# Strassen-like projection groups: the second sum of weight quarters made by an adding DMA onto the first quarter's tile, with three of the sums of h negated

## The chip, the cores and the metric

The kernel runs on one core of one Trainium2 chip. The metric is the device time of one execution in microseconds (us); the figures are the median of three runs and, for everything read from the trace, one profiled execution. The engines are PE (matrix products), DVE (vector), ACT (scalar), POOL (general purpose, here used mostly to issue adding DMAs) and SP (issues the plain loads). TensorE's granted clock is given as a share of its full level of 2.4 GHz.

## The reference

The input x has 512 rows of 1024 channels. One layer: an RMS norm, one large projection with w_in (1024 to 12 x 1024 columns), three parallel branches, a gated merge, an output projection and a last norm.

```python
h = rmsnorm(x, norm_g[l])
proj = jnp.einsum('bsd,dn->bsn', h, w_in[l])
a_u, a_v, a_z, b_p, b_z, c_h, c_b, c_c, c_z, gate_logits = jnp.split(proj, SPLIT_OFFSETS, axis=-1)
ya = spatial_gating(gelu(a_u), gelu(a_v), ...) * silu(a_z)
yb = multiscale_pool(b_p, ...) * silu(b_z)
yc = c_b * causal_depthwise_conv(c_c * c_h, conv_w[l], conv_b[l]) * silu(c_z)
merged = sum over the branches of sigmoid(gate) * einsum(y, w_branch)
x = x + einsum(merged, w_out[l]);  return rmsnorm(x, final_g)
```

## The kernel before

**Products.** fp32 values are split into a high part (`whi`, `b11h`, made by a cast on ACT, line 59) and a rest (`wlo`, `b11l`, made by a subtraction on DVE, line 60); a product is three PE passes, high x high, high x rest, rest x high.

**Groups.** Eleven of the twelve blocks of 1024 columns of w_in (all but a_v) are computed in two groups each, 22 in all, by the generator `group`. A group has 2 x 256 output columns (halves `nh`) and the whole contraction of 1024 (halves `kh`), for 512 tokens (halves T1, T2). It takes seven products of quarter size instead of eight (a scheme of Strassen's kind). The fixed operands are quarters of h and their sums, made once by `sum_form`: b11, b21, b22, t1, t2, t3, t4. The weights are quarters `a11`, `a12`, `a21`, `a22` of 512 KB and sums of them. One product (`product`, line 444) is 24 matmuls of 256 columns on a weight tile of 128 x 1024.

**Order within a group.** `run` interleaves the groups: the first product of the next group (b11) stands ahead of the last two of this one (b22, t4). In the order of the code: b11 | b21, t2, t1, t3 | (b11 of the next group) b22, t4. The PSUM bank px takes b11, t2, t3 and t4 in turn; after each of the first three it is copied out by ACT (`copied`, line 450) before the next product is added to it. The order of each engine's instructions is fixed when the kernel is built, by a scheduler that keeps to the dependences and the buffers.

**Weights.** SP loads a11, a12, a21, a22 into tiles of the pool `wraw` (7 buffers, line 64) and the quarter (0,1) once more into `s1` (pool `wsum`, 2 buffers, line 468); POOL issues a DMA that adds the quarter (1,1) onto s1 in flight (line 469). DVE makes the other sums in place (line 457): a21 = a11 - a21, a11 = s1 - a11, a12 = a12 - a11. Every weight tile is then split by ACT and DVE into `whi` and `wlo`, which have 4 buffers each, so that the split of a product can begin when the product four places ahead of it has been read by PE.

**The rest.** Groups are mixed with other products (`proj`, matmuls of 512 columns, lines 105 to 107), with pooling windows (lines 677 to 684) and the convolution (lines 763 to 766) on DVE and ACT. The output projection at the end (lines 800 to 899) already makes its weight sums with adding DMAs (line 813).

Of the kernel before, what the change touches and what calls it, by code (L numbers as in the profile page):

```python
# [16 lines left out]
S = 512  # L17
# [13 lines left out]
def mixers_kernel(ctx, tc, x, norm_g, w_in, sgu_ln_g, sgu_ln_b, sgu_w, sgu_b, pool_w, pool_b, pool_scale,  # L31
# [22 lines left out]
    def bank():  # L54
        return psum.tile([P, 512], F32, tag="ps", name="ps")
# [284 lines left out]

    def sum_form(name, tag, out, in0, in1):
        nc.vector.tensor_tensor(out=out, in0=in0, in1=in1, op=ALU.subtract)
        moving[name] = form_tile(name, tag)
        split(*moving[name], out)


    sum_form("t1", "f3", b11, b12, b11)
    sum_form("t3", "f4", b12, b22, b12)
    sum_form("t2", "f5", b22, b22, b11)


# [48 lines left out]

    sum_form("t4", "f6", b21, b21, b22)

# [20 lines left out]
    def pair_of(ap):  # L423
        return ap.rearrange("p (j t) -> p j t", j=2)

    def group(c0, g, ct, use=None):
# [4 lines left out]
        def quarter(kh, nh):  # L431
            return load_raw(source(kh, nh), [4, GC])
# [19 lines left out]

        def plus(half, ts, s, ps):
            nc.vector.tensor_tensor(out=ct[:, half, :, ts], in0=pair_of(ps), in1=s, op=ALU.add)  # L454

        def sub(out, in0, in1, op=ALU.subtract):
            nc.vector.tensor_tensor(out=out, in0=in0, in1=in1, op=op)  # L457

        a11 = quarter(0, 0)
        f = halved(a11)  # L460
        px, py, pz = bank(), None, None
        product(f, "b11", px, True)
        yield
        c1 = copied(px)
        a12 = quarter(1, 0)
        f = halved(a12)
        s1 = wsum.tile([P, 4, GC], F32, tag="wsum", name="s1")
        nc.sync.dma_start(out=s1, in_=source(0, 1))
        nc.gpsimd.dma_start(out=s1, in_=source(1, 1), accum_op=ALU.add)  # L469
        a21, a22 = quarter(0, 1), quarter(1, 1)  # L470
        py = bank()
        product(f, "b21", py, True)
        plus(0, T1, c1, py)
        sub(a21, a11, a21)
        sub(a11, s1, a11)
        product(halved(a11), "t2", px, False)
        c2 = copied(px)
        pz = bank()
        product(halved(s1), "t1", pz, True)
        product(halved(a21), "t3", px, False)  # L480
        c3 = copied(px)
        sub(a12, a12, a11)
        plus(1, T2, c3, pz)
        yield
        product(halved(a12), "b22", pz, False)
        plus(0, T2, c2, pz)
        if use:
            use(ct[:, 0], 0, slice(0, S))
            use(ct[:, 1, :, T2], 1, T2)
        product(halved(a22), "t4", px, False)  # L490
        if use:
            use(pair_of(px), 1, T1)
        else:
            nc.scalar.copy(out=ct[:, 1, :, T1], in_=pair_of(px))
        yield

    def run(items):
# [22 lines left out]
        finish()  # L520

    def act_into(ct, func):
        def use(src, half, ts):
            nc.scalar.activation(out=ct[:, half, :, ts], in_=src, func=func)
        return use
# [216 lines left out]
    def branch_c(g):  # L742
# [6 lines left out]
        def conv_in():  # L749
            c["cc"] = out_tile("cc")  # L750

            def use(src, half, ts):
                nc.vector.tensor_mul(out=pads[half][:, :, PAD + ts.start : PAD + ts.stop], in0=src,
                                     in1=c["ch"][:, half, :, ts])

            yield from group(OFF["cc"], g, c["cc"], use)
# [12 lines left out]
        def gate_in():  # L769
            c["cb"] = out_tile("cb")  # L770

            def use(src, half, ts):
                y1 = c["cc"][:, half, :, ts]
                nc.vector.tensor_mul(out=y1, in0=src, in1=y1)

            yield from group(OFF["cb"], g, c["cb"], use)
# [27 lines left out]
    def source(n, k, u):  # L804
        r = k * HALF + u * 2 * P
        return w_out[r : r + 2 * P, n * HALF : (n + 1) * HALF].rearrange("(k p) c -> p k c", p=P)
# [118 lines left out]
```

## Time and profile before

| | |
|---|---|
| median of 3 runs | 702.57 us (701.31 to 703.35) |
| the profiled execution | 701.71 us |
| its span in the trace | 699.9 us |
| PE busy | 684.6 us (98%), weight loads 637.2 us (91%) |
| DVE, ACT, POOL busy | 530.6 us (76%), 343.3 us (49%), 53.4 us (8%) |
| mean granted clock of TensorE | 0.996 |

The span runs from the first to the last instruction of the trace; about 2 us of the execution lie around it. Busy time of an engine is the time in which it has an instruction under way; for PE, whose matmuls overlap, it says only that there was always one in flight.

### The profile page before, as it was taken

Reading aid. Unit: us, or ns where it says so; the run is one execution under the profiler, and the core shown is the slowest. Engines: PE = TensorE matmul, PEld = TensorE weight load, DVE = VectorE, ACT = ScalarE, POOL = GpSimd, SP = SyncE. Lnnn points to the kernel's source line nnn. Section 1 sums busy time; section 2 is a strip of 40 time slices with the busy share of each in tenths; the row PEclk is TensorE's granted clock in tenths of the full one; section 3 lists DMA queues with packets and bytes.
Section 4 is the critical chain, followed back from the end, with each engine's and each line's share of the span. In section 5 each row is a group of like instructions: output and inputs, shape, how many; then the busy total and the mean of one; then the engine's idle time right before and its main releaser. Section 6 shows DMA issues by size and latency. Waiting matters only on the chain.

```text
span 699.9 us, 11608 instructions
## 1 busy us (share of the span) xinstructions
PE 684.6 (98%) x4814; PEld 637.2 (91%) x4814; DVE 530.6 (76%) x615; ACT 343.3 (49%) x417; POOL 53.4 (8%) x68
## 2 busy tenths in 40 slices
PE   8999999999999999989999999999999999999994
PEld 6779999999899899989989899999999999898883
DVE  6997679695669667995855666798869975646995
ACT  7543546664244344655614334555645465244553
POOL 3112000000000000000000000000000000002112
PEclk9999999999999999999999999999999999999998
DMA  7974344746265434627617235556665543278733
GB/s 275 309 169 120 121 122 102 213 109 181 79 163 152 149 87 132 175 90 195 197 32 209 91 104 167 149 144 167 176 168 163 163 140 124 81 270 189 149 60 121
DMA packets 94457, 105.12 MB, mean 150 GB/s; under 512 B 3324, under 2 KB 85316, under 8 KB 94404
## 3 DMA queue, kind: packets, MB, share of 16 engines
q1 hardware_dynamic: 80020, 87.60, 38.9%
q0 software_dynamic: 13792, 15.73, 14.4%
q10 hardware_dynamic: 592, 1.05, 0.4%
q8 instruction: 37, 0.61, 0.4%
q14 instruction: 16, 0.13, 0.1%
HBM read 102.27 MB, written 2.10 MB: 149 GB/s over the span
## 4 chain that ended last, share of the span: by engine, by line
PE 89%; DVE 5%; DMA 2%; ACT 1%; issue 1%; POOL 0%; SPq 0%; POOLq 0%; ACTq 0%; DVEq 0%
PE ps L444 58%; PE ps L106 8%; PE ps L107 8%; PE ps L105 8%; PE ps L833 5%; PE ps L265 2%; DVE wlo L60 1%; DMA x_in<-in_x 1%; DVE win L677 1%; DMA wraw<-in_w_in 1%; DVE wraw L457 1%; PE ps L563 1%; PE ps L215 0%; DVE sz L454 0%; DVE ylo L709 0%
## 5 line engine op out<-in xcount | busy, mean ns | idle before, releaser
L59 ACT CAST whi<-wraw 128x1024 fp32r<-128x1024 f32 (+1 forms) x174 | 180.6, 1040 | 262.0 <-PE ps L444 160.2
L60 DVE TENSOR_TENSOR wlo<-wraw,whi 128x1024 fp32r<-128x1024 f32 (+1 forms) x174 | 209.6, 1210 | 95.6 <-ACT whi L59 95.3
L105 PE MATMUL ps<-yhi,whi 128*128 128x512 f32 x208 | 81.0, 389 | 0.0
L107 PE MATMUL ps<-yhi,wlo 128*128 128x512 f32 x208 | 80.9, 389 | 0.0
L106 PE MATMUL ps<-ylo,whi 128*128 128x512 f32 x208 | 80.9, 389 | 0.0
L457 DVE TENSOR_TENSOR wraw<-wraw 128x1024 f32<-128x1024 f32 x44 | 53.4, 1220 | 16.3 <-DMA wraw<-in_w_in 16.3
L469 POOL DMA_DIRECT2D s<-in_w_in x22 | 28.8, 1308 | 482.1 <-DMA s<-in_w_in 81.9
L444 PE MATMUL ps<-b22h,whi 128*128 128x256 f32 x176 | 50.6, 288 | 0.5 <-DVE sz L454 0.5
L444 PE MATMUL ps<-b21h,wlo 128*128 128x256 f32 x176 | 49.4, 280 | 1.2 <-DVE wlo L60 1.2
L444 PE MATMUL ps<-t2h,wlo 128*128 128x256 f32 x176 | 49.4, 281 | 0.5 <-DVE wlo L60 0.5
L444 PE MATMUL ps<-t1h,whi 128*128 128x256 f32 x176 | 49.4, 281 | 0.4 <-ACT whi L59 0.4
L444 PE MATMUL ps<-t2h,whi 128*128 128x256 f32 x176 | 49.5, 281 | 0.1
L444 PE MATMUL ps<-t2l,whi 128*128 128x256 f32 x176 | 49.6, 282 | 0.0
L444 PE MATMUL ps<-b11l,whi 128*128 128x256 f32 x176 | 49.6, 282 | 0.0
L444 PE MATMUL ps<-t3l,whi 128*128 128x256 f32 x176 | 49.6, 282 | 0.0
L444 PE MATMUL ps<-t1l,whi 128*128 128x256 f32 x176 | 49.6, 282 | 0.0
L444 PE MATMUL ps<-b22l,whi 128*128 128x256 f32 x176 | 49.6, 282 | 0.0
L444 PE MATMUL ps<-t4l,whi 128*128 128x256 f32 x176 | 49.6, 282 | 0.0
L444 PE MATMUL ps<-b21l,whi 128*128 128x256 f32 x176 | 49.6, 282 | 0.0
L444 PE MATMUL ps<-t3h,whi 128*128 128x256 f32 x176 | 49.3, 280 | 0.0
L444 PE MATMUL ps<-b22h,wlo 128*128 128x256 f32 x176 | 49.3, 280 | 0.0
L444 PE MATMUL ps<-b21h,whi 128*128 128x256 f32 x176 | 49.3, 280 | 0.0
(224 smaller groups left out, 1849.6 us busy)
## 6 DMA issues: line engine op xcount, KB each, us to landing
wraw<-in_w_in SPq DMA_DIRECT2D x96, 512.0 KB, 4.0
s<-in_w_in SPq DMA_DIRECT2D x22, 512.0 KB, 3.6
s<-in_w_in POOLq DMA_DIRECT2D x22, 512.0 KB, 6.3
wraw<-in_w_out SPq DMA_DIRECT2D x10, 512.0 KB, 3.8
wraw<-in_w_branch_a SPq DMA_DIRECT2D x8, 512.0 KB, 3.7
wraw<-in_w_branch_b SPq DMA_DIRECT2D x8, 512.0 KB
wraw<-in_w_branch_c SPq DMA_DIRECT2D x8, 512.0 KB
wraw<-in_w_out POOLq DMA_DIRECT2D x8, 512.0 KB, 6.0
```

Of the source, the lines that this page charges most:

```text
L59: keep(nc.scalar.copy(out=hi, in_=src))
L60: keep(nc.vector.tensor_tensor(out=lo, in0=src, in1=hi.bitcast(F32), op=ALU.subtract))
L105: nc.tensor.matmul(ps, lhsT=a[0], rhs=b[0], start=first, stop=False)
L106: nc.tensor.matmul(ps, lhsT=a[0], rhs=b[1], start=False, stop=False)
L107: nc.tensor.matmul(ps, lhsT=a[1], rhs=b[0], start=False, stop=last)
L265: pin(nc.tensor.matmul(vps[b], lhsT=a, rhs=r, start=done[b] == 1, stop=done[b] == 3 * KT))
L444: nc.tensor.matmul(ps[:, j * GC : (j + 1) * GC], lhsT=a[x][:, k, j * P : (j + 1) * P], rhs=moving[b][y][:, k, :], start=first and j == 0 a ...
L457: nc.vector.tensor_tensor(out=out, in0=in0, in1=in1, op=op)
L469: nc.gpsimd.dma_start(out=s1, in_=source(1, 1), accum_op=ALU.add)
L563: nc.tensor.matmul(mx[:, n * P : (n + 1) * P], lhsT=v_t[:, n, t * P : (t + 1) * P], rhs=wsT[:, t, :], start=True, stop=True)
L677: nc.vector.tensor_add(out=nxt[:, lo:], in0=cur[:, lo:], in1=cur[:, lo - step : PAD + S - step])
L833: nc.tensor.matmul(pss[b], lhsT=m_form[name][x_][:, k, b * P : (b + 1) * P], rhs=(hi, lo)[y_][:, k % 2, :], start=first and k == 0 and n == 0,
```

## The change

The group makes its second sum by a DMA too. s1 = (0,1) + (1,1) is used first, with -t1. DVE then adds a11 to s1 in place (line 481), which gives the operand for -t2, and adds that to a12 (line 486). When DVE has read a11, POOL issues a DMA that adds the quarter (0,1) from memory onto a11's tile (line 482); the tile then holds the operand for t3. The quarter a21 is no longer loaded into a tile of its own. Signs: the weight sums are now sums instead of differences, so t1, t2 and t4 are made with the opposite sign, and the uses of one output quarter get a sign (`plus`, `times`, `act_into`, a `scalar.mul` in place of a copy). The order of the products in the code is b21, -t1, -t2, t3 instead of b21, t2, t1, t3. Per group there are two DVE operations on weights instead of three, four loads by SP instead of five, and two adding DMAs instead of one.

```diff
@@ -338,15 +338,19 @@
     b11, b12, b22, b21 = (hsum[:, i] for i in range(4))
     moving = {"b11": hq[0, 0], "b21": hq[1, 0], "b22": hq[1, 1]}
 
-    def sum_form(name, tag, out, in0, in1):
-        nc.vector.tensor_tensor(out=out, in0=in0, in1=in1, op=ALU.subtract)
+    def sum_form(name, tag, out, in0, in1, sign=1.0):
+
+        if sign == 1.0:
+            nc.vector.tensor_tensor(out=out, in0=in0, in1=in1, op=ALU.subtract)
+        else:
+            nc.vector.scalar_tensor_tensor(out=out, in0=in0, scalar=sign, in1=in1, op0=ALU.mult, op1=ALU.subtract)
         moving[name] = form_tile(name, tag)
         split(*moving[name], out)
 
 
-    sum_form("t1", "f3", b11, b12, b11)
+    sum_form("-t1", "f3", b11, b11, b12)
     sum_form("t3", "f4", b12, b22, b12)
-    sum_form("t2", "f5", b22, b22, b11)
+    sum_form("-t2", "f5", b22, b22, b11, -1.0)
 
 
     ws_bs = outs.tile([P, 2, KT, P], F32, tag="outs", name="ws_bs")
@@ -398,7 +402,7 @@
         nc.vector.tensor_scalar(out=v_t[:, b, :], in0=v_t[:, b, :], scalar1=mv[:, 0:1], scalar2=rv,
                                 op0=ALU.subtract, op1=ALU.mult)
 
-    sum_form("t4", "f6", b21, b21, b22)
+    sum_form("-t4", "f6", b21, b22, b21, -1.0)
 
     def proj(w, j, rhs_hi, rhs_lo, nk=KT):
         ps = bank()
@@ -450,48 +454,50 @@
             nc.scalar.copy(out=s, in_=ps)
             return pair_of(s)
 
-        def plus(half, ts, s, ps):
-            nc.vector.tensor_tensor(out=ct[:, half, :, ts], in0=pair_of(ps), in1=s, op=ALU.add)
-
-        def sub(out, in0, in1, op=ALU.subtract):
-            nc.vector.tensor_tensor(out=out, in0=in0, in1=in1, op=op)
+        def plus(half, ts, s, ps, sign=1.0):
+            o = ct[:, half, :, ts]
+            if sign == 1.0:
+                nc.vector.tensor_tensor(out=o, in0=pair_of(ps), in1=s, op=ALU.add)
+            else:
+                nc.vector.scalar_tensor_tensor(out=o, in0=pair_of(ps), scalar=sign, in1=s, op0=ALU.mult,
+                                               op1=ALU.subtract)
 
         a11 = quarter(0, 0)
         f = halved(a11)
-        px, py, pz = bank(), None, None
+        px = bank()
         product(f, "b11", px, True)
         yield
         c1 = copied(px)
-        a12 = quarter(1, 0)
-        f = halved(a12)
         s1 = wsum.tile([P, 4, GC], F32, tag="wsum", name="s1")
         nc.sync.dma_start(out=s1, in_=source(0, 1))
         nc.gpsimd.dma_start(out=s1, in_=source(1, 1), accum_op=ALU.add)
-        a21, a22 = quarter(0, 1), quarter(1, 1)
+        a12 = quarter(1, 0)
+        f = halved(a12)
         py = bank()
         product(f, "b21", py, True)
         plus(0, T1, c1, py)
-        sub(a21, a11, a21)
-        sub(a11, s1, a11)
-        product(halved(a11), "t2", px, False)
+        pz = bank()
+        product(halved(s1), "-t1", pz, True)
+        nc.vector.tensor_tensor(out=s1, in0=s1, in1=a11, op=ALU.add)
+        nc.gpsimd.dma_start(out=a11, in_=source(0, 1), accum_op=ALU.add)
+        product(halved(s1), "-t2", px, False)
         c2 = copied(px)
-        pz = bank()
-        product(halved(s1), "t1", pz, True)
-        product(halved(a21), "t3", px, False)
+        a22 = quarter(1, 1)
+        nc.vector.tensor_tensor(out=a12, in0=a12, in1=s1, op=ALU.add)
+        product(halved(a11), "t3", px, False)
         c3 = copied(px)
-        sub(a12, a12, a11)
-        plus(1, T2, c3, pz)
+        plus(1, T2, c3, pz, 1.0 if use else -1.0)
         yield
         product(halved(a12), "b22", pz, False)
         plus(0, T2, c2, pz)
         if use:
-            use(ct[:, 0], 0, slice(0, S))
-            use(ct[:, 1, :, T2], 1, T2)
-        product(halved(a22), "t4", px, False)
+            use(ct[:, 0], 0, slice(0, S), 1.0)
+            use(ct[:, 1, :, T2], 1, T2, -1.0)
+        product(halved(a22), "-t4", px, False)
         if use:
-            use(pair_of(px), 1, T1)
+            use(pair_of(px), 1, T1, -1.0)
         else:
-            nc.scalar.copy(out=ct[:, 1, :, T1], in_=pair_of(px))
+            nc.scalar.mul(out=ct[:, 1, :, T1], in_=pair_of(px), mul=-1.0)
         yield
 
     def run(items):
@@ -519,9 +525,15 @@
                     after()
         finish()
 
+    def times(out, in0, in1, sign):
+        if sign == 1.0:
+            nc.vector.tensor_mul(out=out, in0=in0, in1=in1)
+        else:
+            nc.vector.scalar_tensor_tensor(out=out, in0=in0, scalar=sign, in1=in1, op0=ALU.mult, op1=ALU.mult)
+
     def act_into(ct, func):
-        def use(src, half, ts):
-            nc.scalar.activation(out=ct[:, half, :, ts], in_=src, func=func)
+        def use(src, half, ts, sign):
+            nc.scalar.activation(out=ct[:, half, :, ts], in_=src, func=func, scale=sign)
         return use
 
     def y_tiles():
@@ -749,9 +761,8 @@
         def conv_in():
             c["cc"] = out_tile("cc")
 
-            def use(src, half, ts):
-                nc.vector.tensor_mul(out=pads[half][:, :, PAD + ts.start : PAD + ts.stop], in0=src,
-                                     in1=c["ch"][:, half, :, ts])
+            def use(src, half, ts, sign):
+                times(pads[half][:, :, PAD + ts.start : PAD + ts.stop], src, c["ch"][:, half, :, ts], sign)
 
             yield from group(OFF["cc"], g, c["cc"], use)
 
@@ -769,9 +780,9 @@
         def gate_in():
             c["cb"] = out_tile("cb")
 
-            def use(src, half, ts):
+            def use(src, half, ts, sign):
                 y1 = c["cc"][:, half, :, ts]
-                nc.vector.tensor_mul(out=y1, in0=src, in1=y1)
+                times(y1, src, y1, sign)
 
             yield from group(OFF["cb"], g, c["cb"], use)
 
```

How it stands in the engines' order. All three places are in branch c, between the groups of block cc and block cb. ACT: s1_4386 is the weight sum of cc's group, wraw_4295 its a11, wraw_4389 its a12, wraw_4482 its a22; wraw_4517 is a11 of cb's group, and `part` tiles are copies of px. First the change:

```order
L59 CAST whi_4422<-s1_4386 128x1024
L454 COPY part_4384<-ps_4301 128x512
L59 CAST whi_4452<-s1_4386 128x1024
L500 ACTIVATE ch_4130<-ps_4137 128x2x256
L59 CAST whi_4485<-wraw_4295 128x1024
L59 CAST whi_4519<-wraw_4517 128x1024
L59 CAST whi_4548<-wraw_4389 128x1024
L59 CAST whi_4579<-wraw_4482 128x1024
L454 COPY part_4480<-ps_4301 128x512
```

and before (s1_4418, wraw_4321, wraw_4421 and wraw_4412 are the sum, a11, a21 and a12 of cc's group; wraw_4545 is a11 of cb's):

```order
L59 CAST whi_4453<-wraw_4321 128x1024
L450 COPY part_4410<-ps_4327 128x512
L59 CAST whi_4484<-s1_4418 128x1024
L59 CAST whi_4512<-wraw_4421 128x1024
L494 COPY ch_4154<-ps_4161 128x2x256
L59 CAST whi_4547<-wraw_4545 128x1024
L59 CAST whi_4576<-wraw_4412 128x1024
L450 COPY part_4481<-ps_4327 128x512
```

In the change the cast of the tile that the new DMA writes (whi_4485) stands ahead of the cast for the next group's first product (whi_4519) and of two more, and the copy of px after -t2 (part_4480) stands behind all of them; before, the tile wraw_4421 in that place was a DVE result.

PE at the same place. ps_4301 is px of cc's group, ps_4523 that of cb's; before they are ps_4327 and ps_4551, and ps_4483 is pz. The change, at the end of -t2:

```order
L448 MATMUL ps_4301<--t2h_433,whi_4452 128x256
L448 MATMUL ps_4301<--t2l_434,whi_4452 128x256
L448 MATMUL ps_4301<--t2h_433,wlo_4453 128x256
L448 MATMUL ps_4523<-b11h_163,whi_4519 128x256
L448 MATMUL ps_4523<-b11l_164,whi_4519 128x256
L448 MATMUL ps_4523<-b11h_163,wlo_4520 128x256
L448 MATMUL ps_4523<-b11h_163,whi_4519 128x256
```

and before, at the end of t1:

```order
L444 MATMUL ps_4483<-t1h_423,whi_4484 128x256
L444 MATMUL ps_4483<-t1l_424,whi_4484 128x256
L444 MATMUL ps_4483<-t1h_423,wlo_4485 128x256
L444 MATMUL ps_4327<-t3h_428,whi_4512 128x256
L444 MATMUL ps_4327<-t3l_429,whi_4512 128x256
L444 MATMUL ps_4327<-t3h_428,wlo_4513 128x256
```

Before, t1 with its 24 rows lies between t2 and t3, which share a bank, and the next group's b11 comes after t3. In the change b11 comes right behind -t2, and after 13 rows of it the 24 rows of t3 follow, then the other 11 of b11. From the first row of one b11 to that of the next there are 168 rows; the last row of b11 is the 48th, and -t1 begins with the 121st, -t2 with the 145th.

DVE one group later: cb's weight sum s1_4622, and the convolution (L775, L777; before L764, L766) of the block cc. The change:

```order
L532 SCALAR_TENSOR_TENSOR ppad1_1961<-cc_4294,ch_4130 128x2x256
L481 TENSOR_TENSOR s1_4622<-s1_4622,wraw_4517 128x1024
L486 TENSOR_TENSOR wraw_4625<-wraw_4625,s1_4622 128x1024
L460 TENSOR_TENSOR cc_4294<-ps_4421,part_4480 128x2x256
L532 SCALAR_TENSOR_TENSOR ppad1_1961<-ps_4301,ch_4130 128x2x256
L530 TENSOR_TENSOR ppad0_1959<-cc_4294,ch_4130 128x2x512
L775 SCALAR_TENSOR_TENSOR cc_4294<-ppad1_1961,pvec_442,cc_4294 128x512 x2
L775 SCALAR_TENSOR_TENSOR cc_4294<-ppad0_1959,pvec_442,cc_4294 128x512 x2
L777 SCALAR_TENSOR_TENSOR cc_4294<-ppad0_1959,pvec_442,cc_4294 128x512 x2
L777 SCALAR_TENSOR_TENSOR cc_4294<-ppad1_1961,pvec_442,cc_4294 128x512 x2
L460 TENSOR_TENSOR cb_4516<-ps_4631,part_4620 128x2x256
L60 TENSOR_TENSOR wlo_4689<-s1_4622,whi_4688 128x1024
```

and before (s1_4656 and wraw_4659 are the sum and a21 of cb's group, wraw_4783 is a11 of cz's):

```order
L454 TENSOR_TENSOR cc_4320<-ps_4483,part_4481 128x2x256
L60 TENSOR_TENSOR wlo_4723<-s1_4656,whi_4722 128x1024
L753 TENSOR_TENSOR ppad0_1969<-cc_4320,ch_4154 128x2x512
L753 TENSOR_TENSOR ppad1_1971<-ps_4327,ch_4154 128x2x256
L60 TENSOR_TENSOR wlo_4751<-wraw_4659,whi_4750 128x1024
L764 SCALAR_TENSOR_TENSOR cc_4320<-ppad0_1969,pvec_442,cc_4320 128x512 x2
L766 SCALAR_TENSOR_TENSOR cc_4320<-ppad0_1969,pvec_442,cc_4320 128x512 x2
L764 SCALAR_TENSOR_TENSOR cc_4320<-ppad1_1971,pvec_442,cc_4320 128x512 x2
L766 SCALAR_TENSOR_TENSOR cc_4320<-ppad1_1971,pvec_442,cc_4320 128x512 x2
L454 TENSOR_TENSOR cb_4544<-ps_4663,part_4648 128x2x256
L60 TENSOR_TENSOR wlo_4786<-wraw_4783,whi_4785 128x1024
L60 TENSOR_TENSOR wlo_4815<-wraw_4650,whi_4814 128x1024
```

Before, the rests for t1 and t3 of cb's group (wlo_4723, wlo_4751) stand ahead of the convolution's eight operations; in the change the rest for -t2 (wlo_4689) and the three behind it stand after them.

## Rows read from the trace of the kernel before

**Rows 1.** The page: span, and busy time by engine (share of the span) and instructions
```profile
span 699.9 us, 11608 instructions
PE 684.6 (98%) x4814; PEld 637.2 (91%) x4814; DVE 530.6 (76%) x615; ACT 343.3 (49%) x417; POOL 53.4 (8%) x68
```

**Rows 2.** Five stretches of 10 us: busy time by engine, clock, DMA share and rate
```profile
core 0: us, PE busy (x) PEld busy (x) DVE busy (x) ACT busy (x) POOL busy (x), PEclk, DMA share, GB/s
90.00:100.00 10.00, 9.51 (x82) 9.32 (x81) 5.77 (x6) 5.63 (x7) 0.63 (x1) 1.00 0.67 157
290.00:300.00 10.00, 10.00 (x77) 9.53 (x76) 10.00 (x17) 6.88 (x10) 0.00 (x0) 1.00 0.20 63
300.00:310.00 10.00, 7.79 (x60) 6.96 (x59) 9.93 (x12) 5.51 (x7) 0.00 (x0) 1.00 0.11 28
430.00:440.00 10.00, 10.00 (x87) 10.00 (x87) 7.10 (x7) 4.60 (x6) 1.30 (x1) 1.00 0.69 186
460.00:470.00 10.00, 10.00 (x87) 10.00 (x87) 10.00 (x12) 5.03 (x6) 0.00 (x0) 1.00 0.64 152
```

**Rows 3.** Chain that ended last: a run of group matmuls (start, us)
```profile
337.73 5.65 PE ps L444 x48
```

**Rows 4.** ACT in time order: start, us, [idle before <-releaser]
```profile
429.43 1.05 ACT L59 CAST whi<-s 128x1024 fp32r<-128x1024 f32 x1 [1.57 <-PE ps L444]
432.14 1.05 ACT L59 CAST whi<-wraw 128x1024 fp32r<-128x1024 f32 x1 [1.66 <-PE ps L444]
433.09 0.58 ACT L494 COPY ch<-ps 128x512 f32<-128x512 f32 x1
```

**Rows 5.** PE in time order, the end of a product
```profile
429.11 0.28 PE L444 MATMUL ps<-b22l,whi 128*128 128x256 f32 x1
```

**Rows 6.** DVE in time order, around the convolution
```profile
449.14 1.22 DVE L457 TENSOR_TENSOR wraw<-wraw 128x1024 f32<-128x1024 f32 x1
450.27 0.69 DVE L454 TENSOR_TENSOR cc<-ps,part 128x512 f32<-128x512 f32 x1
450.87 1.22 DVE L60 TENSOR_TENSOR wlo<-s,whi 128x1024 fp32r<-128x1024 f32 x1
452.01 1.22 DVE L753 TENSOR_TENSOR ppad<-cc,ch 128x1024 f32<-128x1024 f32 x1
453.14 0.68 DVE L753 TENSOR_TENSOR ppad<-ps,ch 128x512 f32<-128x512 f32 x1
453.74 1.22 DVE L60 TENSOR_TENSOR wlo<-wraw,whi 128x1024 fp32r<-128x1024 f32 x1
454.87 1.41 DVE L764 SCALAR_TENSOR_TENSOR cc<-ppad,pvec,cc 128x512 f32<-128x512 f32 x2
456.20 1.41 DVE L766 SCALAR_TENSOR_TENSOR cc<-ppad,pvec,cc 128x512 f32<-128x512 f32 x2
```

**Rows 7.** Adding DMAs onto s1, 410 to 450 us
```profile
L469 POOL DMA_DIRECT2D s<-in_w_in x2: 1292/1296/1301, 416.4 to 436.1; - x2
DMA to landing us min/median/max: 5.9/5.9/6.0
```

**Rows 8.** Adding DMAs onto s1, 110 to 170 us
```profile
L469 POOL DMA_DIRECT2D s<-in_w_in x3: 1294/1297/1306, 115.4 to 158.1; - x3
DMA to landing us min/median/max: 9.6/10.1/10.5
```

**Rows 9.** The page, DMA issues: count, KB each, median us from issue to landing
```profile
s<-in_w_in SPq DMA_DIRECT2D x22, 512.0 KB, 3.6
s<-in_w_in POOLq DMA_DIRECT2D x22, 512.0 KB, 6.3
```

**Rows 10.** DVE in time order, before an adding DMA
```profile
650.25 1.23 DVE L60 TENSOR_TENSOR wlo<-wraw,whi 128x1024 fp32r<-128x1024 f32 x1 [1.09 <-ACT whi L59]
```

**Rows 11.** POOL in time order, that adding DMA
```profile
651.84 1.20 POOL L813 DMA_DIRECT2D wraw<-in_w_out  x1 [6.15 <-DVE wlo L60]
```

**Rows 12.** The page: the three weight sums' line on DVE
```profile
L457 DVE TENSOR_TENSOR wraw<-wraw 128x1024 f32<-128x1024 f32 x44 | 53.4, 1220 | 16.3 <-DMA wraw<-in_w_in 16.3
```

## The prediction

> **What bounds the kernel now.** I read the page first: of a span of 699.9 us PE has a matmul in flight for 684.6 us [rows 1]. Then the stretches of 10 us: PE shows 10.00 of 10.00 in all but a few between 25 us and the end, at a granted clock of 1.00. The lacks that matter are 0.49 us at 90 to 100 and 2.21 us at 300 to 310, where DVE is full [rows 2]: 2.7 us together. So what the change can give back is 2.7 us; a saving of work on DVE, SP or the DMA engines is worth nothing elsewhere. What it can take is any wait that it puts in front of PE. A matmul of 256 columns costs PE 5.65/48 = 0.118 us [rows 3], a product of 24 costs 2.83 us, and a group's seven 19.8 us.
>
> How far do the splits run ahead? The casts on ACT wait for PE [rows 4], and the one at 429.43 starts 0.04 us after the end (429.11 + 0.28) of the last reader of the tile whose buffer it takes [rows 5]. That is the rule of four buffers: the split of a product can start three products, 8.5 us, before its own product does. Before the change this covers a cast of 1.05 us and a subtraction of 1.22 us [rows 4, 6] with ease. After it, a DMA has to fit in as well.
>
> **What goes.** One DVE sum per group: 22 x 1.14 us (the distance from one such operation to the next [rows 6]) = 25 us of 530.6 [rows 1], beside a PE that is full, so nothing but a part of the 2.7 us. The line of the sums waited 16.3 us for loads [rows 12], most of it behind PE too. One plain load per group goes and one adding DMA comes; the bytes are the same. The signs cost nothing that lasts: `scalar_tensor_tensor` on 512 columns takes what `tensor_tensor` takes (1.41 for two against 0.69 for one [rows 6]). On POOL, two of layer norm's small powers now stand behind the first new DMA; what they feed is first read by the products of line 563, two groups or 40 us later.
>
> **What comes: the chain of the second sum.** I follow it once, from cc to cb in branch c, with 0 at the first matmul of b11, by the rows shown with the change. All in us.
> b11's last row, the 48th, ends at 5.65 + 0.2; with the hand-over below, the cast for -t1 starts at 6.1 and ends at 7.15. The rest for -t1 on DVE finds a 512-column sum (0.60) half done and ends at 8.7. The sum onto s1 ends at 9.85. POOL starts an adding DMA 0.36 after the DVE operation that it waits for (650.25 + 1.23 against 651.84 [rows 10, 11]): 10.2. Landing took 5.9 in an undisturbed stretch [rows 7]: 16.1. The cast for t3 ends at 17.2 and that for the next b11, behind it in ACT's queue, at 18.1. On DVE the rest for t3 is followed by a sum (0.60) and the rest for b11, which ends at 17.2 + 1.14 + 0.60 + 1.22 = 20.2.
> PE wants the cast for b11 with row 169, at 19.8, and the rest two rows later at 20.0; with two hand-overs, 20.3. So the chain just fits, with about 0.1 to spare on DVE and 2 on ACT, and whatever the landing takes above 5.9 is paid on PE, since t3 stands ahead of b11 in both queues. Over all 22 adding DMAs of before the median is 6.3 [rows 9]; in the change the next s1 load comes free when the rest for -t2 is done, about 12.4, in the middle of the landing. I take 6.4, a wait of 0.4 per group.
>
> The Trainium skill, "DMA: Bandwidth & Descriptors", section on the anatomy of one DMA on the SWDGE path, gives about 2.0 us plus the bytes over 436e3 per us, which is 3.2 us for these 512 KB; the trace disagrees, with 5.9 [rows 7]. By 3.2 the chain would have 2.7 to spare.
>
> **Hand-over of px.** Before, t1 lay between t2 and t3, and the copy of px had a whole product's time. Now 13 rows of b11 (1.53) lie between, and ACT makes the cast for -t4 first (0.95), then the copy (0.58 [rows 4]): the copy ends 0.20 + 0.95 + 0.58 + 0.04 = 1.77 after the last row of -t2 has started, and the 13 rows and that one last 1.65. So 0.12, and the same once more between t3 and -t4; I take 0.3 per group.
>
> **Where DVE is busy with other work.** Three kinds of place:
> - The convolution, twice (both groups of cb): from the end of the rest for -t1, at 8.7, stand 0.60 + 1.14 + 1.14 + 0.60 + 0.60 + 1.13, eight operations at 1.33 for two (454.87 to 456.20 [rows 6]), 0.60 and the rest for -t2, 1.22: it ends at 21.0. PE wants it at its 149th row (two of b11 stand in between), 17.4 + 0.3. A wait of 3.3, where before this stretch was full on PE (460 to 470 us, [rows 2]); 6.6 for both.
> - Branch a, twice: the two products of 1024 columns that finish az stand between the rest for -t1 and the sum, 2.3 late; 2.1 each, 4.2.
> - The second group of bz, behind the pooling windows, where DVE is full before (290 to 310 us, [rows 2]) and late against PE: the sum then ends about when -t1 ends. From its end to the cast for b11 are 0.36 + 5.9 + 0.97 + 1.05, or 8.3 us, and PE has -t2 left, 2.83 plus its own wait of about 1: some 5.
>
> **Sum.** The other 17 or so groups at 0.3 + 0.4 make 12; with 6.6, 4.2 and 5 that is 27.8; less the 2.7 of before, which these waits swallow, 25. The profiled execution took 701.7 us, 1.8 of it around the span and unchanged: 726.7. It lies 0.9 below the median of three runs, inside their spread of 2 us; I say 726. The granted clock I leave at 1.00, as in the stretch where PE was busy 7.79 of 10 [rows 2]. Bounds of the one price that no row of this place shows, the landing on a11's tile: below, the plain load's 3.6 us [rows 9]; above, the 10.1 of a stretch with other loads about [rows 8]. I stay near 5.9 because SP issues fewer loads per group than before.
>
> **Rivals.**
> - *The DMA lands like a plain load, at 3.6.* Then the 0.4 of 17 groups and branch a's waits vanish and bz keeps 2.7: 701.7 + 5.1 + 6.6 + 2.7 - 2.7 = 713. For it: the same bytes. Against: 22 adding DMAs with a median of 6.3 [rows 9]. By the skill's fit, named above, it would be this case.
> - *It lands late, at 10.1.* SP's loads of the next group share the DMA engines with it; each of some 20 groups pays 10.1 - 5.9 = 4.2, less 0.3 of hand-over: 78 on top of the rest, about 790; half as often, 760. For it: [rows 8]. Against: [rows 7].
> - *Faster.* The saved DVE time decides: if the sum onto s1 ends some 1 us earlier than I place it, because DVE no longer does a21 ahead of it, the chain has spare everywhere but at the convolution, and if that stretch is earlier too, the 2.7 us come back: 699. It decides once every rest is ready 3 us before PE. Against: DVE was not what delayed it; the cast waits for PE's buffer [rows 4].
> - *No change*: the same with the convolution's waits against the 2.7, 701 to 704.
>
> **Chances.** The forecast 0.68 (715 to 746), early landing 0.12 (707 to 715), late landing 0.08, faster 0.06, no change 0.06. A measurement here tells about 0.3%, 2 us, from nothing. Range 707 to 746: the forecast's spread is 1 us of landing either way, worth about 20 us upward, and the lower case; it leaves out the faster, the unchanged and the late case, 0.2. Faster 0.06, same 0.06, slower 0.88.
>
> **What will show it.** PE busy 25 us or so short of the span's middle, with waits named ACT whi or DVE wlo in front of line 448. ACT waiting for a DMA onto wraw in front of the cast for t3, in most groups. 22 rows of line 482 on POOL, each about 6 us from issue to landing and starting 10 us after b11's first row. Two waits of about 3 us on PE in branch c behind the convolution's rows. DVE near 506 us. It would be wrong if the cast for t3 finds its data there, or if landings lie at 10.

## The result, and the profile after

The changed kernel takes 739.77 us (738.90 to 741.13, four runs) against 702.96 us: a ratio of 1.053, interval 1.0506 to 1.0554. That is 37 us slower, inside the predicted range of 707 to 746 and 14 above the predicted 726.

The page of the changed kernel, its span, the busy time of the engines, the new adding DMA's line and its DMA issues; they answer to [rows 1, 9, 12]:

```profile
span 738.0 us, 11582 instructions
...
PE 702.9 (95%) x4814; PEld 647.4 (88%) x4814; DVE 504.0 (68%) x593; ACT 340.1 (46%) x417; POOL 81.2 (11%) x90
...
L482 POOL DMA_DIRECT2D wraw<-in_w_in x22 | 28.5, 1295 | 374.7 <-DVE s L481 127.4
...
wraw<-in_w_in SPq DMA_DIRECT2D x74, 512.0 KB, 6.2
...
s<-in_w_in POOLq DMA_DIRECT2D x22, 512.0 KB, 7.5
wraw<-in_w_in POOLq DMA_DIRECT2D x22, 512.0 KB, 5.8
```

DVE has 26 us less, about what the change promised. The span is longer by 38 us, and PE's busy time by 18 although it has the same 4814 matmuls, so not all of the loss is idle time of PE: matmuls also followed each other more slowly. The chain of waits shows the new wait on ACT:

```profile
ACT whi L59 <- DMA wraw<-in_w_in: 79.8, 20, 6.6
```

ACT now waits for a landing in front of 20 casts, up to 6.6 us and 79.8 us in all. For a group in which nothing else goes on, the timeline of three engines:

```profile
437.81 0.28 PE L448 MATMUL ps<-b11h,whi 128*128 128x256 f32 x1
...
448.52 1.29 POOL L482 DMA_DIRECT2D wraw<-in_w_in  x1 [11.39 <-issue]
...
454.40 2.00 ACT L59 CAST whi<-wraw 128x1024 fp32r<-128x1024 f32 x2 [3.80 <-DMA wraw<-in_w_in]
...
458.04 0.28 PE L448 MATMUL ps<-b11h,whi 128*128 128x256 f32 x1
458.15 0.28 PE L448 MATMUL ps<-b11l,whi 128*128 128x256 f32 x1
458.49 0.39 PE L448 MATMUL ps<-b11h,wlo 128*128 128x256 f32 x1
```

The DMA starts 10.7 us after the first row of b11 (the prediction said 10.2), ACT waits 3.8 us for it, its two casts for t3 and b11 end at 456.4, and PE, which wants b11 at 458.04, loses only 0.22 us, at the rest of b11 two rows later. The chain just fits, as worked out. It does not fit at a branch's end. The timeline of the changed kernel there:

```profile
608.04 1.06 ACT L59 CAST whi<-wraw 128x1024 fp32r<-128x1024 f32 x1 [2.82 <-DMA wraw<-in_w_in]
609.00 1.99 ACT L59 CAST yhi<-cz 128x1024 fp32r<-128x1024 f32 x2
...
610.07 2.36 DVE L60 TENSOR_TENSOR ylo<-cz,yhi 128x1024 fp32r<-128x1024 f32 x2 [2.34 <-ACT yhi L59]
612.35 4.62 DVE L60 TENSOR_TENSOR wlo<-wraw,whi 128x1024 fp32r<-128x1024 f32 x4
...
614.76 0.76 PE L107 MATMUL ps<-yhi,wlo 128*128 128x512 f32 x1 [2.04 <-DVE wlo L60]
```

The casts of the branch's result (`yhi`) stand on ACT behind the cast for t3, which waits for the landing; DVE then makes `ylo` and the rests one after the other, and PE waits 2.04 us for a weight that has nothing to do with the DMA.

What slowed the matmuls is in the windows of the changed kernel. Of all stretches of 10 us between 20 and 730, these are the ones with a granted clock (third figure from the right) under 0.99:

```profile
160.00:170.00 10.00, 7.92 (x49) 6.86 (x49) 6.70 (x6) 4.37 (x5) 1.30 (x1) 0.88 0.72 170
170.00:180.00 10.00, 10.00 (x67) 9.32 (x66) 2.04 (x3) 3.74 (x5) 0.00 (x0) 0.95 0.95 250
320.00:330.00 10.00, 6.61 (x41) 6.41 (x40) 4.72 (x4) 4.37 (x5) 1.30 (x1) 0.73 0.68 145
330.00:340.00 10.00, 10.00 (x79) 9.86 (x79) 6.44 (x7) 5.60 (x7) 1.29 (x1) 0.92 0.56 144
470.00:480.00 10.00, 7.21 (x56) 6.79 (x55) 10.00 (x14) 5.88 (x7) 0.52 (x1) 0.91 0.35 54
480.00:490.00 10.00, 10.00 (x67) 9.96 (x65) 3.85 (x4) 2.51 (x4) 1.30 (x1) 0.74 0.95 252
610.00:620.00 10.00, 7.96 (x47) 7.04 (x46) 6.90 (x6) 4.31 (x6) 0.00 (x0) 0.83 0.46 142
```

Four times the clock falls behind a wait of PE, and at 170, 330 and 480 PE is busy for all 10.00 us, at half its clock for a part of them. In the kernel before, every stretch of 10 us from 20 to 690 us has 1.00; its last matmul starts at 690.5. The rows of PE at the first group of cb show the fall, and windows of 2 us how long it lasts:

```profile
475.58 0.28 PE L448 MATMUL ps<--t2h,whi 128*128 128x256 f32 x1
475.69 0.28 PE L448 MATMUL ps<--t2l,whi 128*128 128x256 f32 x1
477.79 0.39 PE L448 MATMUL ps<-b11h,whi 128*128 128x256 f32 x1 [1.81 <-ACT whi L59]
478.01 0.28 PE L448 MATMUL ps<-b11l,whi 128*128 128x256 f32 x1
479.27 0.58 PE L448 MATMUL ps<--t2h,wlo 128*128 128x256 f32 x1 [0.98 <-DVE wlo L60]
479.65 0.42 PE L448 MATMUL ps<--t2h,whi 128*128 128x256 f32 x1
479.87 0.41 PE L448 MATMUL ps<--t2l,whi 128*128 128x256 f32 x1
```

```profile
476.00:478.00 2.00, 0.21 (x1) 0.21 (x2) 2.00 (x4) 2.00 (x3) 0.00 (x0) 1.00 0.00 0
478.00:480.00 2.00, 1.02 (x5) 0.81 (x5) 2.00 (x3) 0.69 (x1) 0.00 (x0) 0.57 0.00 0
480.00:482.00 2.00, 2.00 (x11) 2.00 (x10) 2.00 (x3) 0.00 (x0) 0.00 (x0) 0.50 0.73 231
482.00:484.00 2.00, 2.00 (x11) 2.00 (x11) 0.63 (x1) 0.00 (x0) 0.35 (x1) 0.50 0.88 283
484.00:486.00 2.00, 2.00 (x15) 2.00 (x15) 0.71 (x1) 1.53 (x2) 0.96 (x1) 0.72 0.87 263
486.00:488.00 2.00, 2.00 (x19) 2.00 (x18) 0.51 (x1) 0.00 (x0) 0.00 (x0) 1.00 1.16 192
```

Ahead of the wait matmuls start 0.12 us apart, behind it 0.22 us: 1.2 GHz instead of 2.4, for some 7 us. The Trainium skill, "TensorE: Matmul & The Clock Gate", Part 1, says that the clock has these two levels and goes by how busy PE has been lately; the trace agrees on the levels, 0.50 and 1.00.

For all kernels below I took the start of each matmul to the start of the next from PE's rows, from 46 us on, and set the 0.118 us of 256 columns (0.233 of 512) against it. What a distance of over 2.15 times that lies above it is counted as a wait. The last column is the most that the lower clock can have cost: for every stretch of 10 us from 20 us until the matmuls end, 10 us times what its granted clock lacks to 1.00, added up. Both in us:

| kernel | time | ratio to before | waits | lower clock, at most |
|---|---|---|---|---|
| before | 702.96 | | 3.4 | 0 |
| changed | 739.77 | 1.053 | 29.2 | 10.4 |
| a21 loaded plainly, DVE sum (e1) | 724.49 | 1.0298 | 17.5 | 5.1 |
| adding DMA on a fresh copy (e2) | 719.02 | 1.0219 | 13.2 | 5.1 |
| five split buffers (e3) | 720.48 | 1.0236 | 13.3 | 5.1 |
| five raw buffers alone (g3) | 739.73 | 1.0515 | 26.6 | 11.9 |
| chain 1.2 us longer (e4) | 762.71 | 1.0837 | 46.6 | 13.6 |
| changed, -t1 behind -t2 (f1) | 724.49 | 1.0298 | 17.5 | 6.8 |
| e2, -t1 behind -t2 (f2) | 703.68 | 1.0004 | 3.6 | 0 |
| e2, convolution later (f3) | 710.58 | 1.0108 | 7.9 | 0 |
| e2, rows in the wait (f4) | 715.75 | 1.0188 | 7.1 | 0 |
| before, t1 and t2 swapped (g1) | 724.12 | 1.0312 | 14.7 | 6.8 |
| f1, sum on its own tile (g2) | 704.90 | 1.0033 | 5.2 | 1.7 |
| g2, one sum moved (h1) | 705.30 | 1.0021 | 5.7 | 1.7 |

A part of a stretch at the lower clock is wait anyway. In the changed kernel the matmuls that start inside these stretches lie 7.4 us above their distance at the full clock. So the 38.1 us between the two spans (738.0 and 699.9) are 25.8 of waits, 7.4 of lower clock, about 4 of shorter lags at the full clock (hand-overs of px, and the row behind a wait) and 1 that the groups start later.

### The profile page after: what moved, and what is told of

The parts are those of the page before. It is cut to its first block, busy times and chain, and to the rows that moved or that the text cites. A ratio compares the mean times of both kernels' runs of the same rounds, so it can differ in the third digit from the quotient of the medians.

```text
span 738.0 us, 11582 instructions
## 1 busy us (share of the span) xinstructions
PE 702.9 (95%) x4814; PEld 647.4 (88%) x4814; DVE 504.0 (68%) x593; ACT 340.1 (46%) x417; POOL 81.2 (11%) x90
## 5 line engine op out<-in xcount | busy, mean ns | idle before, releaser
L59 ACT CAST whi<-s 128x1024 fp32r<-128x1024 f32 x44 | 46.3, 1052 | 82.9 <-PE ps L106 35.5
L60 DVE TENSOR_TENSOR wlo<-s,whi 128x1024 fp32r<-128x1024 f32 x44 | 53.6, 1218 | 13.7 <-ACT whi L59 13.7
L448 PE MATMUL ps<-b11h,whi 128*128 128x256 f32 x176 | 50.2, 285 | 7.6 <-ACT whi L59 7.6
L448 PE MATMUL ps<--t2h,wlo 128*128 128x256 f32 x176 | 50.7, 288 | 3.4 <-DVE wlo L60 3.4
L448 PE MATMUL ps<-b11h,wlo 128*128 128x256 f32 x176 | 50.1, 284 | 3.3 <-DVE wlo L60 3.2
L107 PEld LDWEIGHTS ps<-yhi,wlo 128*128 128x128 f32 x208 | 39.4, 189 | 13.6 <-DVE wlo L60 5.8
L448 PE MATMUL ps<--t4h,whi 128*128 128x256 f32 x176 | 50.8, 289 | 0.0
L448 PE MATMUL ps<-t3h,wlo 128*128 128x256 f32 x176 | 50.8, 289 | 0.0
L448 PE MATMUL ps<--t2h,whi 128*128 128x256 f32 x176 | 50.3, 286 | 0.3 <-ACT whi L59 0.3
L448 PE MATMUL ps<--t2l,whi 128*128 128x256 f32 x176 | 50.5, 287 | 0.0
L448 PE MATMUL ps<--t1l,whi 128*128 128x256 f32 x176 | 49.6, 282 | 0.0
```

What stands on the lines that cost most here:

```text
L59: keep(nc.scalar.copy(out=hi, in_=src))
L60: keep(nc.vector.tensor_tensor(out=lo, in0=src, in1=hi.bitcast(F32), op=ALU.subtract))
L107: nc.tensor.matmul(ps, lhsT=a[1], rhs=b[0], start=False, stop=last)
L448: nc.tensor.matmul(ps[:, j * GC : (j + 1) * GC], lhsT=a[x][:, k, j * P : (j + 1) * P], rhs=moving[b][y][:, k, :], start=first and j == 0 a ...
```

## Experiments

My theory was the chain: the second adding DMA starts behind DVE's sum, lands 5.8 us later, and the cast for t3, with all behind it on ACT, waits. The rivals were the order of the products with its signs, and the traffic of the DMAs.

**e1: the second adding DMA taken out.**

```diff
+        a21 = quarter(0, 1)
         py = bank()
...
-        nc.gpsimd.dma_start(out=a11, in_=source(0, 1), accum_op=ALU.add)
+        nc.vector.tensor_tensor(out=a11, in0=a11, in1=a21, op=ALU.add)
```

> The changed kernel with its order of products and its signs, but a21 is loaded by itself again and added to a11 on DVE: the second adding DMA is gone. Chain theory (PE waits because the cast for t3, and the cast for the next b11 behind it on ACT, stand behind sum, adding DMA and landing): the waits go, the twenty hand-overs of px at 0.13 us stay (2.6 us), at the convolution a part of the 1.15 us waits for the rest of -t2 may stay; 704 to 710 us, granted clock back at 0.99 or more, ACT's waits for a DMA onto wraw in front of line 59 from 79.8 us to under 25. Rival, order and signs (the product order, the hand-overs and the signed sums cost the time, not the DMA): 733 to 740 us.

724.49 us, ratio 1.0298 (1.0250 to 1.0346): between both expectations, so both missed. Without the DMA 15 of the 37 us go and 22 stay, so the chain theory alone was wrong.

**e2: the adding DMA kept, but onto a second copy of the first quarter**, so that it waits for no sum.

```diff
+        a21 = quarter(0, 0)
+        nc.gpsimd.dma_start(out=a21, in_=source(0, 1), accum_op=ALU.add)
         py = bank()
...
-        nc.gpsimd.dma_start(out=a11, in_=source(0, 1), accum_op=ALU.add)
...
-        product(halved(a11), "t3", px, False)
+        product(halved(a21), "t3", px, False)
```

> The changed kernel, but the adding DMA goes onto a second copy of the first quarter, which SP loads by itself, so that it waits for no sum on DVE and starts several us earlier; one load more per group than in the changed kernel, as many adding DMAs, one DVE sum fewer than before. Chain theory: it is the start of the DMA behind the sum that costs, not the DMA: 704 to 710 us, DVE near 505 us of busy time, clock 0.99 or more. Rival, traffic (two adding DMAs a group are slow, or they delay the loads): above 725 us, and more than the changed kernel if the bytes decide.

719.02 us, ratio 1.0219 (1.0168 to 1.0270), between the 704 to 710 of the chain theory and the 725 of its rival. It moves 11.5 MB more than the changed kernel (22 loads of 512 KB) and is 21 us faster: traffic falls as a cause, the late start of the DMA is one, and something else is left. Of the waits left, 6.6 us are the two groups of cb. The timeline of e2 at the first:

```profile
457.15 2.81 DVE L776 SCALAR_TENSOR_TENSOR cc<-ppad,pvec,cc 128x512 f32<-128x512 f32 x4
459.88 2.73 DVE L778 SCALAR_TENSOR_TENSOR cc<-ppad,pvec,cc 128x512 f32<-128x512 f32 x4
462.53 0.68 DVE L460 TENSOR_TENSOR cb<-ps,part 128x512 f32<-128x512 f32 x1
463.13 1.21 DVE L60 TENSOR_TENSOR wlo<-s,whi 128x1024 fp32r<-128x1024 f32 x1
...
464.40 0.58 PE L448 MATMUL ps<--t2h,wlo 128*128 128x256 f32 x1 [3.15 <-DVE wlo L60]
```

The rest for -t2 stands behind the eight operations of the convolution, as the prediction laid it out, and PE waits 3.15 us (3.3 was forecast). This is order on DVE, not the DMA.

**e3 and g3: buffers.** e3 has five split buffers for four, and for their room five raw ones for seven; g3 has the five raw ones alone.

```diff
-    wraw = ctx.enter_context(tc.tile_pool(name="wraw", bufs=7))
+    wraw = ctx.enter_context(tc.tile_pool(name="wraw", bufs=5))
...
-    whi = ctx.enter_context(tc.tile_pool(name="whi", bufs=4))
-    wlo = ctx.enter_context(tc.tile_pool(name="wlo", bufs=4))
+    whi = ctx.enter_context(tc.tile_pool(name="whi", bufs=5))
+    wlo = ctx.enter_context(tc.tile_pool(name="wlo", bufs=5))
```

> The changed kernel with five buffers instead of four for the high and for the low halves of the split weights (and five instead of seven for the raw loads, which makes the room). Chain theory: the cast for -t1 and with it the whole chain can start one product, 2.8 us, earlier, which is more than most of the waits: 705 to 716 us, if five raw buffers are enough. Rival, order and signs: nothing changes, 733 to 742 us. Rival, traffic: the same or worse, as the loads have fewer buffers.

> The changed kernel with five raw buffers instead of seven and nothing else, to set beside the run with five split buffers, which had five raw ones too. If the raw buffers don't matter: 737 to 743 us, and the 19 us of that run are the split buffers' doing. If they do: 745 us or more, and the split buffers are worth more than 19 us.

720.48 us, ratio 1.0236 (1.0193 to 1.0279), against 739.73, ratio 1.0515 (1.0475 to 1.0556). One split more of run-ahead, 2.8 us, is worth 19 us; the raw buffers nothing. The theory expected more of it, 705 to 716, and which of the two causes found below the fifth buffer relieves is not separated by these runs. The rule of four buffers, with which the prediction began, is what the chain has to fit into.

**e4: the chain 1.2 us longer.**

```diff
+        nc.vector.tensor_tensor(out=a11, in0=a11, in1=a11, op=ALU.max)
         nc.gpsimd.dma_start(out=a11, in_=source(0, 1), accum_op=ALU.add)
```

> The changed kernel with one DVE operation more (the maximum of a11 with itself, about 1.2 us) between the sum onto s1 and the adding DMA of every group: the chain is 1.2 us longer. As the prediction had it (0.1 us to spare in an ordinary group): every one of some 20 groups pays 1.1 us, 22 us, and the clock a little more: 760 to 768 us. By the trace of the changed kernel, where an ordinary group shows no wait of PE over 0.15 us: ordinary groups have room left, and only the nine or ten places that wait already pay 1.2 us each: 748 to 754 us. Rivals without the chain (order and signs, traffic): DVE is far from full, 739 to 742 us.

762.71 us, ratio 1.0837 (1.0790 to 1.0884): 23 us more, inside the expected 760 to 768. By the distance of 1.14 us from one such operation to the next, 22 of them are 25 us. But the groups do not pay alike. Two ordinary groups in a row pay 1.1 and 0.5 us (by start to start, PE waits 1.11 at 459 and 0.75 at 480 for the rest of b11; in the changed kernel none at 438 and 0.22 at 458), and at three places, at 126, 178 and 346, PE waits 3.7 to 5.1 us for ACT's copy of px. Two rows of the timeline of e4:

```profile
345.61 0.58 PE L448 MATMUL ps<-t3h,whi 128*128 128x256 f32 x1 [4.60 <-ACT part L454]
...
459.46 0.38 PE L448 MATMUL ps<-b11h,wlo 128*128 128x256 f32 x1 [0.95 <-DVE wlo L60]
```

So the ordinary group has little room, though the trace of the changed kernel shows it with next to no wait; that the time came out as if each group had paid the same is in part luck.

**f1, f2 and g1: the order of the products.** f1 is the changed kernel and f2 the kernel e2, both with -t1's product behind -t2's, as it stood before; g1 is the kernel before with t1 and t2 swapped and nothing else.

```diff
         pz = bank()
-        product(halved(s1), "-t1", pz, True)
+        f = halved(s1)
...
         c2 = copied(px)
+        product(f, "-t1", pz, True)
```

> The changed kernel, second adding DMA and signs and all, but with the product of -t1 moved behind that of -t2, as t1 stands behind t2 before. No row of b11 then stands between -t2 and t3, copies of px have a whole product's time, and the buffer that the cast for -t1 takes comes free one product, 2.8 us, earlier. Chain theory with the order as a part of it (the DMA chain costs because this order of products starts it late): the chain ends 2.8 us earlier against PE, which is more than all waits but those at the second group of bz: 703 to 712 us. Rival, the DMA chain alone (t3 is wanted where it was, the landing is late whatever the order): only the hand-overs go, 733 to 738 us.

> The kernel with the adding DMA on a second copy of the first quarter (that of 719 us), and with the product of -t1 moved behind that of -t2. Theory that what is left there is order (the wait of 3.3 us at each convolution, for the rest of -t2 behind DVE's eight operations, the hand-overs of px, and the lower clock behind the waits): 701 to 706 us. Rival, bytes or the signs cost what is left: 715 to 720 us.

> The kernel before, with nothing changed but the places of the products of t1 and t2, which are swapped: b11, b21, t1, t2, t3. No sign is turned, no DMA added, three DVE sums as before. Theory that the order of the products costs 15 to 20 us by itself (13 rows of the next b11 between t2 and t3, the hand-overs of px, the convolution's operations ahead of the rest of t2, the lower clock behind the waits): 716 to 725 us. Rival, the order costs only together with the signed sums or the second adding DMA: 701 to 706 us.

f1: 724.49 us, ratio 1.0298 (1.0271 to 1.0325). f2: 703.68, ratio 1.0004 (0.9990 to 1.0019). g1: 724.12, ratio 1.0312 (1.0271 to 1.0354). The order costs 22 us in the kernel before, without a sign or a DMA changed, the same as in e1, which has that order too; the late DMA costs 22 in the old order; both together 37; neither, nothing. So the two overlap in part. f2 has all the signs, so these cost nothing that shows. f1 missed its expectation of 703 to 712: I had the chain fit everywhere but at the second group of bz. It does not fit in branch a, where 4.4 us of waits stay of the changed kernel's 4.9, nor at the ends of branches; bz keeps 4.8. The timeline of f1 at the last one:

```profile
630.12 1.30 POOL L482 DMA_DIRECT2D wraw<-in_w_in  x1 [41.45 <-DVE pr L631]
...
639.24 2.94 ACT L59 CAST whi<-wraw 128x1024 fp32r<-128x1024 f32 x3 [6.98 <-DMA wraw<-in_w_in]
642.08 0.58 ACT L454 COPY part<-ps 128x512 f32<-128x512 f32 x1
...
642.71 0.52 PE L448 MATMUL ps<-t3h,whi 128*128 128x256 f32 x1 [2.60 <-ACT part L454]
```

This one landing took 9.0 us, beside a 1024 KB load; ACT stood 6.98 us, three casts went ahead of the copy of px, and PE waited 2.60 for the copy. ACT's waiting as such is no measure of the loss: in f1 it waits 82.3 us for landings on wraw, in the changed kernel 79.8, and f1 is 15 us faster.

**f3: the convolution written later**, on e2: `run` holds it back until the next group's t3 is written.

```diff
-                finish()
+                conv = finish(True)
                 next(gen)
+                if conv:
+                    conv()
```

> The kernel of 719 us with its order of products, but the convolution is written behind the next group's t3, so that the rest of -t2 stands ahead of its eight operations on DVE. Theory: the two waits of 3.3 us and the clock behind them (some 5 us) go, the hand-overs stay: 706 to 710 us. Rival, DVE's order is not what PE waits for there: 717 to 720 us; rival, the wait goes but the clock falls all the same: 712 to 714 us.

710.58 us, ratio 1.0108 (1.0086 to 1.0130), just above the expected 706 to 710. The waits of 3.3 us are gone, and with them the lower clock; a new one of 1.43 stands at each of the two places, in front of t3.

**f4: rows in the wait**, on e2: 24 matmuls ahead of the third row of -t2 in the groups of cb. They add work and take none away.

```diff
+                        if row == 2 and fill:
+                            spare = bank()
+                            for _ in range(fill):
+                                pin(nc.tensor.matmul(spare[:, 0:GC], lhsT=moving["b11"][0][:, 0, 0:P],
+                                                     rhs=moving["b11"][0][:, 0, :], start=True, stop=True))
```

> The kernel of 719 us with 24 matmuls more, into a bank that nobody reads, in front of the third row of -t2 in each of the two groups of cb, where PE waits 3.3 us: they take 2.8 us of that wait and no work is taken away. Theory that the lower granted clock behind the wait costs by itself: the waits stay but the clock stays at 1.00 behind them, and some 5 us come back: 713 to 715 us. Rival, the clock falls for another reason, or costs nothing, as PE waits for others anyway: 718 to 720 us, and 721 or more where the added rows are in the way.

715.75 us, ratio 1.0188 (1.0159 to 1.0217). That is between the theory's 713 to 715 and the rival's 718. The intervals of f4 and e2 overlap, so the times alone don't decide; the windows do. First e2, then f4:

```profile
460.00:470.00 10.00, 6.85 (x37) 6.65 (x36) 7.75 (x9) 1.83 (x3) 1.20 (x1) 0.68 0.40 122
...
550.00:560.00 10.00, 8.40 (x56) 8.20 (x57) 6.17 (x6) 1.53 (x2) 1.29 (x1) 0.83 0.78 230
```

```profile
460.00:470.00 10.00, 9.70 (x80) 9.30 (x79) 9.44 (x11) 3.27 (x4) 0.69 (x1) 1.00 0.35 109
...
550.00:560.00 10.00, 9.99 (x80) 9.39 (x80) 6.02 (x6) 4.01 (x5) 1.29 (x1) 1.00 0.78 228
```

With PE occupied in the wait the clock stays at 1.00, and the at most 5.1 us of lower clock in the table go; the span is 3.3 us shorter (716.6 to 713.3) with 48 matmuls more. So the lower clock behind a wait is a cost of its own.

**g2 and h1: both causes removed without an extra load.** g2 is f1 with s1 + a11 written to a tile of its own as soon as s1 has landed; h1 moves one of these sums on DVE.

```diff
+        s2 = wsum.tile([P, 4, GC], F32, tag="wsum", name="s2")
+        nc.vector.tensor_tensor(out=s2, in0=s1, in1=a11, op=ALU.add)
+        nc.gpsimd.dma_start(out=a11, in_=source(0, 1), accum_op=ALU.add)
         a12 = quarter(1, 0)
...
-        nc.vector.tensor_tensor(out=s1, in0=s1, in1=a11, op=ALU.add)
-        nc.gpsimd.dma_start(out=a11, in_=source(0, 1), accum_op=ALU.add)
-        product(halved(s1), "-t2", px, False)
+        product(halved(s2), "-t2", px, False)
```

> The changed kernel with -t1 behind -t2, and with s1 + a11 written to a tile of its own as soon as s1 has landed, so that the sum doesn't wait for the split of -t1 and the second adding DMA starts that much earlier; no load is added (a third sum tile takes the place of one of seven raw buffers). Theory that the two causes are the order and the late start of the second adding DMA, and that PE bounds what is left: 701 to 705 us with DVE near 505 us busy. If the saved 25 us of DVE were worth something: 697 to 700 us. Rival, a second adding DMA on a tile that is in use is slow wherever it starts: 715 us or more.

> The kernel of 704.9 us (sum on a tile of its own, -t1 behind -t2), with one DVE operation moved: the sum for the third group, which stood on DVE ahead of the second group's rest of -t2 and waited 7.66 us for its data there, now stands behind that rest. Theory that this one wait of PE (4.24 us and the lower clock behind it, some 1.7 us) is what keeps that kernel above the one before, and that its freer DVE stretch at 300 to 310 us gives back 2 us: 698 to 701 us, faster than before by 0.2 to 0.6%. Rival, the wait comes back elsewhere on the same queue, or PE bounds it at the same time: 702 to 705 us.

g2: 704.90 us, ratio 1.0033 (1.0020 to 1.0046), with DVE at 506.5 us. The chain's waits are gone (ACT waits for a landing on wraw 3 times, 8.5 us in all, instead of 20 times and 79.8), and so is the lack of 2.21 us at 300 to 310 [rows 2]. A window and two rows of the timeline of g2:

```profile
300.00:310.00 10.00, 10.00 (x76) 9.50 (x75) 9.91 (x15) 8.39 (x12) 1.08 (x1) 1.00 0.40 71
```

```profile
132.86 1.22 DVE L475 TENSOR_TENSOR s<-s,wraw 128x1024 f32<-128x1024 f32 x1 [7.66 <-issue]
...
135.88 0.58 PE L448 MATMUL ps<--t2h,wlo 128*128 128x256 f32 x1 [4.08 <-DVE wlo L60]
```

One long wait is left: the next group's sum stands on DVE ahead of this group's rest for -t2 and waits 7.66 us, to the time at which its s1 lands (the adding DMA started at 127.10 and took 5.7). h1 was to move that sum, and moved the one of the group before: 705.30 us, ratio 1.0021 (1.0008 to 1.0034), with the same wait at 137.32, 4.72 us by start to start. It does not test its theory. Moving the right one was not tried; whether it gives the kernel that beats before stays open.

## Why the prediction was right, and where it was off

The direction, the range and the main mechanism held: a chain that just fits, and an order that puts other work ahead. The size was 14 us short. By its terms, the waits as distances above a matmul's own in the changed kernel:

- **Convolution, 6.6**: 1.98 + 1.14 at 478 and 1.32 + 1.79 at 567, 6.2. Right. The first of each pair is a wait for ACT's cast for b11, behind the landing, and the second for the rest of -t2; in e2 and g1, where no landing is late, the rest alone costs 3.3 at each place, so it is DVE's order that sets the sum.
- **Branch a, 4.2**: 1.36 + 1.11 at 119 and 1.51 + 0.88 at 166, 4.9. Right.
- **The second group of bz, 5**: 0.49 + 0.97 + 3.55 at 318 to 326, 5.0. Right.
- **Ordinary groups, 12**: the hand-overs of px are 17 of 0.12 to 0.14, each with a second lag of 0.10 in the row behind, 4 in all, where 0.3 for each of 17 groups was taken, 5; the 0.4 for a late landing did not come, since 21 of the 22 landed in 5.6 to 6.4 us, median 5.8, as [rows 7] had it, and one in 8.7. The term is 8 too large. The fit of the Trainium skill named in the prediction, 3.2 us, is further off; the measurement decides.
- **Not in the sum**: the ends and beginnings of branches, most of them where ACT and DVE do a branch's own work around the waiting cast for t3: 0.75 at 232, 1.48 at 295, 0.66 at 302, 2.42 at 528, 2.20 at 615, 0.95 and 1.48 at 659 to 661; 9.9 us. The 0.75 is the order's and not the chain's: it stands in e1, e2 and g1 too (0.79, 0.74, 0.79). By luck these 9.9 fill the hole of the term above, so that the 25 forecast for all waits meets 25.8.
- **"The granted clock I leave at 1.00"** is the step that failed. It rested on a single stretch, 300 to 310, whose lacks were of 1.4, 0.6 and 0.7 us. The waits of the change are longer or stand in pairs, the clock fell behind four of them, and 7.4 us by the matmuls' distances, or 9 by the mean clock ((1 - 0.984) x 738.0 less (1 - 0.996) x 699.9), were lost to it: more than half of the 13 us by which the span is longer than forecast. That it is the idle PE in a wait that brings the lower clock, f4 shows.
- **How the cost divides.** The prediction gave the new order of products (hand-overs and convolution) 11.7 us of its waits and the DMA's chain 16. On the chip each costs 22 alone, g1 and f1, clock included, and both together 37. That the order by itself, without any DMA, is as bad as the whole chain was not foreseen.
- **The rival "faster"** asked for the chain to have room. f2 and g2 give it room and end at 1.0004 and 1.0033: 25 us of DVE are worth nothing measurable while PE is full, as the first paragraph of the prediction said.

## What to carry to other kernels

Before an operand's sum goes from an engine to a DMA, lay the whole chain (sum, start, landing, cast) against the run-ahead that the buffers allow, and look at what is queued in order behind the waiting cast, above all where a branch begins or ends. A swap of two products that looks neutral can cost as much as the DMA, here 22 us, since it decides which engine's queue is in the way. Count a long wait of PE at more than its length: behind it the matmuls can run at half the clock for several us.

## What was not expected of the hardware

- The clock fell to 0.50 behind waits of PE of 1.98 and 1.14 us (by start to start) with two matmuls between, and stayed there for some 7 us, but did not behind one of 2.42 us (at 528) nor behind 1.32 and 1.79 us (at 567). In g3, whose products stand in the same order, it did fall behind the like of the first of these, 2.43 us at 526. The window of the changed kernel, then of g3:

```profile
520.00:530.00 10.00, 7.75 (x65) 7.47 (x64) 7.45 (x7) 6.27 (x7) 1.30 (x1) 1.00 0.70 162
```

```profile
520.00:530.00 10.00, 7.73 (x52) 7.42 (x51) 6.90 (x6) 5.88 (x7) 1.30 (x1) 0.83 0.66 150
```

So the length of a wait alone does not decide, and what a kernel loses to the clock changes from one execution to the next: g3 took 733.41 us at a mean clock of 0.992 and 741.30 at 0.978. Which wait lowers it is not settled by these runs.

- From the end of a sum on DVE to the start of POOL's DMA on its tile it took 0.63 us at 469 (467.37 + 1.22 to 469.22), where the rows of before gave 0.36 [rows 10, 11].
- The first adding DMA, onto s1, landed later once a second stood on the same queue: median 7.5 us instead of 6.3 [rows 9]; but in e1, with one adding DMA a group, it took 8.0 as well, so the second DMA is not shown to be the cause.
